# A two-mixer transformer trunk in split fp32: a new order inside mixer B's attention steps

## The chip, the cores and the metric

One core of a Trainium2 chip runs the whole program. The metric is the device time of one execution in microseconds (us); lower is better.

## The reference

The input is a sequence of 1024 tokens of width 1024, and two layers run over it. Layer 0 uses mixer A (attention over a neighbourhood on a grid of tokens), layer 1 uses mixer B (attention with grouped queries: 16 heads of q share 4 heads of k and v). The change is almost wholly in mixer B. Its core, and what surrounds it:

```
for i in range(DEPTH):                       # 2 layers
    h = rms_norm(x, norm_g[i])
    y = mixer_a(h, ...) if i % 2 == 0 else mixer_b(h, ...)
    x = x + y
    g = sigmoid(rms_norm(x, ple_norm_g[i]) @ ple_w_gate[i])
    x = x + g * (p[i] @ ple_w_proj[i])
return rms_norm(x, final_norm_g)

def mixer_b(h, ...):                         # one 128-query block of one head:
    sc = einsum('bkgqd,bksd->bkgqs', qb, k) * scale
    pr = softmax(sc)
    o  = einsum('bkgqs,bksd->bkgqd', pr, v)
    # heads joined, then (o * silu(gate)) @ w_out
```

## The kernel before, in words

Every fp32 factor of a product is split into a high part and a low part, and the products are made with these in fp32r. PE is TensorE, ACT is ScalarE, DVE is VectorE and POOL is GpSimd.

**The steps of mixer B.** Its attention runs through 128 steps, numbered n from 0. A step is one head h, one half hf of the queries and one block t of 128 queries (t from 0 to 3 within a half; the two heads of a pair follow each other). Step n has four pieces:

- `f_S`: four products give the scores of 128 queries against 1024 keys in PSUM (tile `s`, two buffers); then DVE takes the minimum `mn` of each row (the scores have their sign turned).
- `f_E`: ACT makes the exponential of the scores, tile `P` (two buffers), and the row sums.
- `f_T`: PE transposes `P` in two halves of four 128x128 blocks. Each half goes to one of the two PSUM buffers `t`; ACT copies it out as the high part `PTh`, and DVE subtracts to give the low part `PTl`. A buffer `t` is free when its `PTl` is made.
- `f_AV`: for each pair of steps, 16 products of v with the transposed exponentials go into the single PSUM buffer `o`. For each of 8 blocks k of keys there is one with `PTh[:, k]` and one with `PTl[:, k]`; v is the stationary factor in both. At the end of a head (t = 3), `head_end` lists later work: ACT copies half of `o` (line 479), and DVE adds the other half (`join`, line 443), after which the buffer `o` may be written again.

`q_stack` transposes the q of the next pair of heads (four transposes, line 1038) into a buffer `t`; ACT copies it out (line 1040), and later ACT and DVE make the high and low halves `QS` (lines 1047 and 1048). `k_stack` (lines 970 and 973) does the same for k, in steps 48 to 53.

**What sets the order.** The order of each engine's instructions is the order in which the program calls these pieces; each engine takes its own in that order. The loop over `steps` makes a list `att` of pieces, each with a weight. `mix` calls them one by one, and after each it calls `pulse`, which may split another weight (line 217 on ACT, 218 on DVE) and counts down the work that `post` holds for later. After a piece, `mix` also calls dense items (chunks of the projections that fill PE, some 1.4 us each) until their share of all dense work has caught up with the weights so far. So a piece's weight says how much dense work stands behind it. `CB` holds the weights of an even step, `CN` those of an odd one. An even step calls, before the change: `later.tick`, `f_AV` of step n - 1, `f_E` of n + 1, `f_T` of n, `f_S` of n + 2. An odd step calls `later.tick`, `f_T` of n, `f_E` of n + 1, `f_S` of n + 2. `DT` says after how many pulses the last pair of heads has its reciprocals transposed (`across`, line 462), one number for each half hf. In mixer B the transposes use the buffer `o`, in mixer A a buffer `t`.

```
att.append((later.tick, w[0]))
if av:
    att.append((lambda n=n: f_AV(*steps[n - 1]), w[1]))
te = [(lambda n=n: f_T(*steps[n]), w[2])]
if n + 1 < len(steps):
    te.append((lambda n=n: f_E(*steps[n + 1]), w[3]))
if n % 2 == 0:
    te.reverse()
```

Of the kernel before, what the change touches and what calls it, by code (L numbers as in the profile page):

```python
# [21 lines left out]
NT = 8  # L22
# [5 lines left out]
BIG = 1e30  # L28
WSLOTS = 4
CA = (1.0, 0.5, 1.25, 1.0, 0.75)  # L30
CB = (1.25, 1.0, 2.0, 0.5, 1.0)
CN = (1.5, 0.0, 1.0, 1.0, 1.5)
DG, DR, DQ, DY, NP = 1, 2, 2, 1, 8
KT, KN = 2, 4
DO = (2, 3)
DD = ((3, 2), (3, 2))
DT = (5, 2)
FIN = (4, 4)
HOLD = 2
DP = 1  # L40
KD, KS = 3, 4
QD = (2, 5, 8)
QS_AT = 5
QO = (4, 6)
AGE, LAG = 3, 3
YS = (11, 11)
# [108 lines left out]
def trunk(ctx, tc, x, wts, rpb, gains, hgains, mask, rope, out):  # L155
# [145 lines left out]
    def mm(ps, a, b, first, last):  # L301
        pe.matmul(ps, a, b, start=first, stop=last, skip_group_check=True)  # L302
# [554 lines left out]
    def mixer_b(pend):  # L857
        with ExitStack() as es:
# [10 lines left out]
            PTh = one.tile([128, NT, 256], F32R, name="PTh")  # L869
            PTl = one.tile([128, NT, 256], F32R, name="PTl")  # L870
# [9 lines left out]
            KA, KB, V, QT, QST, P, RS, OP = {}, {}, {}, {}, {}, {}, {}, {}  # L880
            later = Later()
# [189 lines left out]
            def f_E(h, hf, t):  # L1071
                ps, mn = P[h, hf, t]
                p = sb.tile([128, 1024], F32, name="P")
                act.activation(p, ps, AF.Exp, bias=mn, scale=-1.0, accum_out=RS[h, hf][:, t:t + 1])  # L1074
                P[h, hf, t] = p

            def f_T(h, hf, t):
                p = P.pop((h, hf, t))
                c = slice((t % 2) * 128, (t % 2) * 128 + 128)
                for b in range(2):  # L1080
                    ps = psT.tile([128, 4, 128], F32, name="t")
                    for i in range(4):
                        k = 4 * b + i
                        pe.transpose(ps[:, i], p[:, k * 128:(k + 1) * 128], ident)  # L1084
                    ks = slice(4 * b, 4 * b + 4)
                    act.activation(PTh[:, ks, c], ps, AF.Copy)  # L1086
                    dve.tensor_tensor(PTl[:, ks, c], ps, PTh[:, ks, c], ALU.subtract)  # L1087
# [4 lines left out]
            def f_AV(h, hf, t):  # L1092
                if t == 1:
                    OP[h, hf] = psO.tile([128, 512], F32, name="o")
                o = OP[h, hf][:, (t - 1) * 128:(t + 1) * 128]
                for k in range(NT):
                    v = V[h // 4][:, k]
                    mm(o, v, PTh[:, k], t == 1 and k == 0, False)
                    mm(o, v, PTl[:, k], False, t == 3 and k == NT - 1)
                if t == 3:  # L1100
                    fin = head_end(sb, h, hf, RS[h, hf], OP.pop((h, hf)), ylive, 1, gg, talloc)
                    if fin:
                        later.add(FIN[1], fin)
# [17 lines left out]
            for g in range(4):  # L1121
                att = []
                for n in range(32 * g, 32 * g + 32):
                    h, hf, t = steps[n]
                    av = n >= 2 and n % 2 == 0
                    w = CB if av else CN
                    att.append((later.tick, w[0]))
                    if av:
                        att.append((lambda n=n: f_AV(*steps[n - 1]), w[1]))
                    te = [(lambda n=n: f_T(*steps[n]), w[2])]  # L1130
                    if n + 1 < len(steps):
                        te.append((lambda n=n: f_E(*steps[n + 1]), w[3]))
                    if n % 2 == 0:
                        te.reverse()
                    att += te
                    if n + 2 < len(steps):
                        att.append((lambda n=n: f_S(*steps[n + 2]), w[4]))
                    m = n + QS_AT
                    if m % 8 == 0 and m < len(steps):
                        hn, fn, _ = steps[m]  # L1140
                        att.append((lambda hn=hn, fn=fn: q_stack(hn // 2, fn), 0.0))
                    if YLOAD_B <= n < YLOAD_B + NT:
                        att.append((lambda t=n - YLOAD_B: load_y(1, t), 0.0))
                if g == 3:
                    att.append((lambda: f_AV(*steps[-1]), CB[1]))
                def gates(p):
                    return [i for hf in range(2) for i in gate_items("bg", p, hf, dalloc, sb, gg)]
                dense = []
                if g > 0:
                    dense += left  # L1150
                if g < 3:
                    qi = q_items(g + 1, pool)
                    kv = kv_items(1, pool) if g == 1 else [None, None]
                    dense += kv[:-2] + qi[:KS] + [k for k in kv[-2:-1] if k] + qi[KS:8] + [k for k in kv[-1:] if k] + gates(2 * g + 1) + qi[8:]
                    left = gates(2 * g + 2)
                else:
                    WQ.cap[3] = 2
                    dense += gates(2 * g + 1) + pp_items(1, dalloc, sb, TAGS_B)
                mix(att, dense, hold=HOLD if g == 3 else 0)
# [169 lines left out]
```

## Time and profile before

| | us |
|---|---|
| runs of the kernel, three | 1572.35, 1569.87, 1572.43 (median 1572.35) |
| the profiled execution | 1569.38 |
| its span, first to last instruction | 1567.6 |
| PE busy in the span | 1522.6 |
| the 128 steps of mixer B, about 791 to 1369 of the span | 578 |

The profiled execution's own time is 1.8 us more than its span, and 3.0 us less than the median of the runs. The clock granted to PE was 0.998 of full over the span, so the kernel runs at the full clock from end to end.

### The profile page before, as it was taken

The numbers are of one execution on the slowest core, as the hardware profiler recorded it, in microseconds if no ns is written. First come the engines' busy times: TensorE is split into PE (matmuls) and PEld (weight loads), VectorE is DVE, ScalarE is ACT, GpSimd is POOL, SyncE is SP. The second block draws the span as 40 slices with busy tenths as digits, with TensorE's granted clock in tenths as the row PEclk, the third lists the DMA queues.
The fourth block names the chain that finished last, engine by engine and source line by source line (L and its number), as shares of the span: only waits on it lengthen the run. The fifth ranks groups of instructions, "written<-read, shape, count | busy, mean of one in ns | idle before, by whom it ended". The sixth has DMA issues, their size and how long they took to land.

```text
span 1567.6 us, 24292 instructions
## 1 busy us (share of the span) xinstructions
PE 1522.6 (97%) x9048; PEld 1328.5 (85%) x9048; DVE 1025.5 (65%) x2062; ACT 871.6 (56%) x1744; POOL 277.3 (18%) x372
## 2 busy tenths in 40 slices
PE   6999999999999999999999999999999999999997
PEld 5888988988988788888988889989899888788886
DVE  6576576477477436547877776777777877625636
ACT  6465465466366522433566776666667767622422
POOL 2111121122112010000312132443132200000023
PEclk9999999999999999999999999999999999999999
DMA  8212122132123972132210111102111213651213
GB/s 273 78 41 74 49 84 78 34 98 78 35 85 95 340 241 67 62 139 90 74 48 21 38 51 41 58 25 68 37 33 42 75 42 112 225 202 54 74 55 128
DMA packets 89861, 138.84 MB, mean 89 GB/s; under 512 B 16912, under 2 KB 55952, under 8 KB 89744
## 3 DMA queue, kind: packets, MB, share of 16 engines
q1 hardware_dynamic: 85136, 122.62, 24.1%
q10 hardware_dynamic: 4608, 14.68, 2.6%
q8 instruction: 71, 1.16, 0.3%
q14 instruction: 46, 0.38, 0.1%
HBM read 104.65 MB, written 36.15 MB: 90 GB/s over the span
## 4 chain that ended last, share of the span: by engine, by line
PE 40%; DVE 7%; ACT 3%; issue 2%; DMA 0%; ACTq 0%; SPq 0%; POOL 0%; DVEq 0%; POOLq 0%
PE d L302 21%; PE o L302 7%; PE t L1084 5%; PE s L302 5%; DVE PTl L1087 2%; DVE mn L1068 1%; ACT PTh L1086 1%; DVE wl L218 1%; PE t L427 1%; ACT wh L217 1%; PE t L1038 0%; ACT P L1074 0%; DVE QS L1048 0%; DVE ss L915 0%; DVE KB L979 0%
## 5 line engine op out<-in xcount | busy, mean ns | idle before, releaser
L302 PE MATMUL d<-wh,HTh 128*128 128x256 f32 (+1 forms) x1096 | 372.5, 340 | 4.6 <-ACT HTh L428 2.1
L302 PE MATMUL d<-wh,HTl 128*128 128x256 f32 (+1 forms) x1096 | 365.8, 334 | 1.6 <-DVE HTl L429 1.5
L302 PE MATMUL d<-wl,HTh 128*128 128x256 f32 (+1 forms) x1096 | 365.3, 333 | 0.0
L1087 DVE TENSOR_TENSOR PTl<-t,PTh 128x512 fp32r<-128x512 f32 x256 | 164.5, 684 | 115.4 <-ACT PTh L1086 114.9
L302 PEld LDWEIGHTS d<-wh,HTh 128*128 128x128 f32 x1096 | 207.9, 190 | 28.0 <-ACT HTh L428 2.7
L302 PEld LDWEIGHTS d<-wh,HTl 128*128 128x128 f32 x1096 | 207.8, 190 | 24.0 <-DVE HTl L429 2.3
L302 PEld LDWEIGHTS d<-wl,HTh 128*128 128x128 f32 x1096 | 208.1, 190 | 21.4
L302 PE MATMUL d<-HTh,wh 128*128 128x512 f32 x504 | 205.9, 409 | 0.0
L302 PE MATMUL d<-HTh,wl 128*128 128x512 f32 x504 | 197.7, 392 | 0.0
L302 PE MATMUL d<-HTl,wh 128*128 128x512 f32 x504 | 197.7, 392 | 0.0
L1074 ACT ACTIVATE P<-s,mn 128x1024 f32<-128x1024 f32 x128 | 142.8, 1115 | 66.2 <-DVE mn L1068 65.1
L302 PE MATMUL o<-PTl,V 128*128 128x256 f32 (+2 forms) x672 | 174.2, 290 | 3.2 <-DVE PTl L1087 2.0
L302 PE MATMUL o<-PTh,V 128*128 128x256 f32 (+2 forms) x672 | 173.0, 288 | 2.3 <-ACT P L1074 1.1
L1086 ACT ACTIVATE PTh<-t 128x512 fp32r<-128x512 f32 x256 | 139.9, 593 | 45.9 <-PE t L1084 45.0
L1068 DVE TENSOR_REDUCE mn<-s 128x1 f32<-128x1024 f32 x128 | 154.8, 1209 | 10.8 <-PE s L302 10.7
L1084 PE MATMUL t<-ident,P 128*128 128x128 f32 x1024 | 137.2, 275 | 8.0 <-DVE PTl L1087 6.6
L218 DVE TENSOR_TENSOR wl<-wstage,wh 128x1024 fp32r<-128x1024 f32 x89 | 115.0, 1298 | 40.9 <-ACT wh L217 40.4
L302 PEld LDWEIGHTS o<-PTl,V 128*128 128x128 f32 x672 | 127.9, 190 | 10.6 <-DVE PTl L1087 6.4
L302 PEld LDWEIGHTS o<-PTh,V 128*128 128x128 f32 x672 | 127.7, 190 | 8.1 <-issue 1.5
L1084 PEld LDWEIGHTS t<-ident,P 128*128 128x128 f32 x1024 | 114.9, 140 | 23.1 <-DVE PTl L1087 16.2
L302 PE MATMUL s<-KA,QS 128*128 128x512 f32 (+2 forms) x384 | 133.6, 402 | 0.0
L302 PE MATMUL s<-KB,QS 128*128 128x512 f32 (+2 forms) x384 | 121.8, 371 | 0.0
(179 smaller groups left out, 2446.8 us busy)
## 6 DMA issues: line engine op xcount, KB each, us to landing
wstage<-in_wts SPq DMA_DIRECT2D x92, 512.0 KB
X<-in_x SPq DMA_DIRECT2D x16, 512.0 KB
pp<-ppD SPq DMA_DIRECT2D x32, 256.0 KB
rb<-rD SPq DMA_DIRECT2D x56, 128.0 KB
ppD<-th SPq DMA_DIRECT2D x20, 256.0 KB
xD<-X SPq DMA_DIRECT2D x8, 512.0 KB
X<-xD SPq DMA_DIRECT2D x8, 512.0 KB
yD0h<-rb SPq DMA_DIRECT2D x14, 256.0 KB
```

Of the source, the lines that this page charges most:

```text
L217: act.activation(hi, s, AF.Copy)
L218: self.rest = lambda: dve.tensor_tensor(lo, s, hi, ALU.subtract)
L302: pe.matmul(ps, a, b, start=first, stop=last, skip_group_check=True)
L427: pe.transpose(ps[:, k], xn[:, (4 * c + k) * 128:(4 * c + k + 1) * 128], ident)
L1068: dve.tensor_reduce(mn, ps, axis=AX.X, op=ALU.min)
L1074: act.activation(p, ps, AF.Exp, bias=mn, scale=-1.0, accum_out=RS[h, hf][:, t:t + 1])
L1084: pe.transpose(ps[:, i], p[:, k * 128:(k + 1) * 128], ident)
L1086: act.activation(PTh[:, ks, c], ps, AF.Copy)
L1087: dve.tensor_tensor(PTl[:, ks, c], ps, PTh[:, ks, c], ALU.subtract)
```

## The change

In an even step the exponential of the next step is called before the products with v. `q_stack` is called one step later than before, directly behind the products with v of an even step, and no longer at the end of an odd step. In `f_AV` all eight products with `PTh` come first and then all eight with `PTl`. The weights of an even step change, so that the dense chunks stand elsewhere. In `DT` the first half's number goes from 5 to 8; this holds for both mixers.

```diff
-CB = (1.25, 1.0, 2.0, 0.5, 1.0)
-CN = (1.5, 0.0, 1.0, 1.0, 1.5)
+CB = (1.25, 0.0, 3.0, 0.5, 1.0)
+CN = (1.5, 1.0, 1.0, 1.5)
-DT = (5, 2)
+DT = (8, 2)
-QS_AT = 5
+QS_AT = 4
...
                 for k in range(NT):
-                    v = V[h // 4][:, k]
-                    mm(o, v, PTh[:, k], t == 1 and k == 0, False)
-                    mm(o, v, PTl[:, k], False, t == 3 and k == NT - 1)
+                    mm(o, V[h // 4][:, k], PTh[:, k], t == 1 and k == 0, False)
+                for k in range(NT):
+                    mm(o, V[h // 4][:, k], PTl[:, k], False, t == 3 and k == NT - 1)
...
-                    h, hf, t = steps[n]
-                    av = n >= 2 and n % 2 == 0
-                    w = CB if av else CN
-                    att.append((later.tick, w[0]))
-                    if av:
-                        att.append((lambda n=n: f_AV(*steps[n - 1]), w[1]))
-                    te = [(lambda n=n: f_T(*steps[n]), w[2])]
-                    if n + 1 < len(steps):
-                        te.append((lambda n=n: f_E(*steps[n + 1]), w[3]))
+                    m = n + QS_AT
+                    later_exp = [lambda n=n: f_E(*steps[n + 1])] if n + 1 < len(steps) else []
+                    turn = lambda n=n: f_T(*steps[n])
                     if n % 2 == 0:
-                        te.reverse()
-                    att += te
+                        fs = [later.tick] + later_exp
+                        w = CB[:len(fs)] if n else (CB[0], CN[2])
+                        if n >= 2:
+                            fs.append(lambda n=n: f_AV(*steps[n - 1]))
+                            w += CB[2:3]
+                        if m % 8 == 0 and m < len(steps):
+                            hn, fn, _ = steps[m]
+                            fs.append(lambda hn=hn, fn=fn: q_stack(hn // 2, fn))
+                            w = w[:-1] + (0.0, w[-1])
+                        fs.append(turn)
+                        w += CB[3:4]
+                    else:
+                        fs = [later.tick, turn] + later_exp
+                        w = CN[:len(fs)]
                     if n + 2 < len(steps):
-                        att.append((lambda n=n: f_S(*steps[n + 2]), w[4]))
-                    m = n + QS_AT
-                    if m % 8 == 0 and m < len(steps):
-                        hn, fn, _ = steps[m]
-                        att.append((lambda hn=hn, fn=fn: q_stack(hn // 2, fn), 0.0))
+                        fs.append(lambda n=n: f_S(*steps[n + 2]))
+                        w += CB[4:] if n % 2 == 0 else CN[3:]
+                    att += zip(fs, w)
```

What it moves on PE, at steps 75 and 76 (in the middle of mixer B; `d` is a dense chunk, `t<-ident,qt` are q's transposes, `o` the products with v, `t<-ident,P` the transposes of an exponential). Before:

```order
L302 MATMUL d<-HTl,wh_10608 128x512
L302 MATMUL d<-HTh,wl_10609 128x512
L1038 MATMUL t<-ident,qt 128x128 x4
L302 MATMUL o<-PTh,V 128x256
L302 MATMUL o<-PTl,V 128x256
L302 MATMUL o<-PTh,V 128x256
L302 MATMUL o<-PTl,V 128x256
```

After the change:

```order
L302 MATMUL d<-HTl,wh_10608 128x512
L302 MATMUL d<-HTh,wl_10609 128x512
L302 MATMUL o<-PTh,V 128x256 x8
L302 MATMUL o<-PTl,V 128x256 x8
L1038 MATMUL t<-ident,qt 128x128 x4
L1084 MATMUL t<-ident,P 128x128 x8
L302 MATMUL s<-KA,QS 128x512 x2
```

The products no longer alternate, and q's transposes have gone from in front of them to behind them, here directly in front of step 76's transposes.

On ACT at steps 67 to 69 (line 1086 copies out a step's transposes, 1074 is an exponential, 1040 copies out q's transposes, 1047 makes the high halves of q, 479 copies out `o`). Before:

```order
L1086 ACTIVATE PTh<-t 128x4x128 x2
L1074 ACTIVATE P,rs<-s,mn 128x1024
L1040 ACTIVATE th<-t 128x512
L1074 ACTIVATE P,rs<-s,mn 128x1024
L1047 ACTIVATE QS<-th 64x512
L1086 ACTIVATE PTh<-t 128x4x128 x2
L479 ACTIVATE Y<-o 64x512
L1047 ACTIVATE QS<-th 64x512
L1086 ACTIVATE PTh<-t 128x4x128 x2
```

After the change:

```order
L1086 ACTIVATE PTh<-t 128x4x128 x2
L1074 ACTIVATE P,rs<-s,mn 128x1024 x2
L1040 ACTIVATE th<-t 128x512
L1086 ACTIVATE PTh<-t 128x4x128 x2
L479 ACTIVATE Y<-o 64x512
L1047 ACTIVATE QS<-th 64x512
L1086 ACTIVATE PTh<-t 128x4x128 x2
L1074 ACTIVATE P,rs<-s,mn 128x1024
L1047 ACTIVATE QS<-th 64x512
```

Both exponentials (68 and 69) now stand in front of q's copy, and the two high halves of q have moved back by one place each.

On PE at the end of mixer B, step 121 (`o<-ident,rb` are the transposed reciprocals of the last pair's first half). Before:

```order
L1084 MATMUL t<-ident,P 128x128 x8
L462 MATMUL o<-ident,rb 128x128 x4
L302 MATMUL s<-KA,QS 128x512 x2
L302 MATMUL s<-KB,QS 128x512 x2
L302 MATMUL o<-PTh,V 128x256
```

After the change:

```order
L302 MATMUL s<-KB,QS 128x512 x2
L302 MATMUL d<-wh_13373,KA 128x512
L302 MATMUL d<-wl_13374,KA 128x512
L302 MATMUL d<-wh_13373,KB 128x512
L302 MATMUL d<-wh_13373,KA 128x512
L302 MATMUL d<-wl_13374,KA 128x512
L302 MATMUL d<-wh_13373,KB 128x512
L462 MATMUL o<-ident,rb 128x128 x4
L302 MATMUL o<-PTh,V 128x256 x8
```

The reciprocals have moved behind the scores and a dense chunk, and now stand directly in front of the products that write the same buffer `o`.

## Rows read from the trace of the kernel before

**Rows 1.** The page: span, and busy time of PE and its weight loads.

```profile
span 1567.6 us, 24292 instructions
PE 1522.6 (97%) x9048; PEld 1328.5 (85%) x9048; DVE 1025.5 (65%) x2062; ACT 871.6 (56%) x1744; POOL 277.3 (18%) x372
```

**Rows 2.** Stages: from:to, length, busy (count) by engine, clock, DMA share, GB/s.

```profile
791.00:1369.00 578.00, 562.62 (x3820) 504.05 (x3819) 430.44 (x686) 407.21 (x753) 138.83 (x216) 1.00 0.19 61
```

**Rows 3.** Waits of weight loads, 791 to 1369: who waited for whom, total, times, longest.

```profile
PEld t L1084 <- DVE PTl L1087: 16.2, 35, 2.1
PEld o L302 <- DVE PTl L1087: 6.4, 15, 1.0
...
PEld t L1038 <- DVE PTl L1087: 1.6, 2, 1.1
...
PEld t L1038 <- POOL Y L514: 1.3, 1, 1.3
```

**Rows 4.** Groups by line, 791 to 1369: busy us, mean ns of one, idle before.

```profile
L302 PE MATMUL o<-PTl,V 128*128 128x256 f32 x511 | 126.6, 286 | 2.7 <-DVE PTl L1087 2.0
L302 PEld LDWEIGHTS o<-PTl,V 128*128 128x128 f32 x511 | 97.4, 191 | 7.4 <-DVE PTl L1087 6.4
```

**Rows 5.** Timeline, products behind step 31: start, length, what, [idle before, releaser].

```profile
926.52 0.28 PE L302 MATMUL o<-PTh,V 128*128 128x256 f32 x1
...
927.49 0.38 PE L302 MATMUL o<-PTl,V 128*128 128x256 f32 x1 [0.69 <-DVE PTl L1087]
...
927.83 0.28 PE L302 MATMUL o<-PTl,V 128*128 128x256 f32 x1
927.95 0.28 PE L302 MATMUL o<-PTh,V 128*128 128x256 f32 x1
```

**Rows 6.** Timeline around the products behind step 21.

```profile
884.04 0.68 DVE L443 SCALAR_TENSOR_TENSOR Y<-o,Y 64x512 f32<-64x512 f32 x1
...
884.87 0.36 PE L302 MATMUL o<-PTh,V 128*128 128x256 f32 x1 [1.12 <-ACT P L1074]
```

**Rows 7.** Timeline, q's transposes behind step 11's scores.

```profile
841.15 1.28 DVE L1087 TENSOR_TENSOR PTl<-t,PTh 128x512 fp32r<-128x512 f32 x2
...
841.89 0.66 PE L1038 MATMUL t<-ident,qt 128*128 128x128 f32 x4 [0.62 <-DVE PTl L1087]
```

**Rows 8.** Timeline, k's transposes directly in front of step 50's.

```profile
1019.82 0.60 PE L970 MATMUL t<-ident,qt 128*128 128x128 f32 x4
1020.25 0.60 PE L1084 MATMUL t<-ident,P 128*128 128x128 f32 x4
1020.51 0.60 ACT L973 ACTIVATE th<-t 128x512 f32<-128x512 f32 x1 [2.01 <-PE t L970]
...
1021.16 0.66 PE L1084 MATMUL t<-ident,P 128*128 128x128 f32 x4 [0.31 <-ACT th L973]
```

**Rows 9.** Groups of ACT by line, 791 to 1369.

```profile
L1074 ACT ACTIVATE P<-s,mn 128x1024 f32<-128x1024 f32 x128 | 142.8, 1115 | 66.2 <-DVE mn L1068 65.1 <-DVE ss L324 0.2
...
L217 ACT ACTIVATE wh<-wstage 128x1024 fp32r<-128x1024 f32 x17 | 17.6, 1049 | 0.0
```

**Rows 10.** Timeline, step 4's last scores and step 5's transposes.

```profile
813.94 0.63 PE L302 MATMUL s<-KB,QS 128*128 128x512 f32 x2
...
814.61 1.15 PE L1084 MATMUL t<-ident,P 128*128 128x128 f32 x7
```

**Rows 11.** Timeline, step 125's transposes.

```profile
1356.49 1.26 PE L1084 MATMUL t<-ident,P 128*128 128x128 f32 x8 [1.27 <-DVE PTl L1087]
```

**Rows 12.** Timeline, step 121: reciprocals and their copy.

```profile
1339.63 0.65 PE L462 MATMUL o<-ident,rb 128*128 128x128 f32 x4 [1.01 <-DVE Y L443]
...
1340.37 0.62 ACT L465 ACTIVATE rb<-o 128x512 f32<-128x512 f32 x1
```

**Rows 13.** Timeline, end of mixer A: reciprocals, then the next products with v.

```profile
532.39 0.60 PE L462 MATMUL t<-ident,rb 128*128 128x128 f32 x4
...
533.74 0.44 PE L302 MATMUL o<-PTh,V 128*128 128x384 f32 x1 [0.75 <-ACT PTh L680]
```

## The prediction

> **What bounds the kernel now.** I read the page first: PE is busy for 97% of the span [rows 1], so time is gained only where PE stops waiting. Then the stages: the 128 steps of mixer B take 578 us, with PE busy for 562.6, DVE for 430 and ACT for 407 [rows 2]. PE is the bound; DVE and ACT, at about 72%, are not, but they hand PE its buffers in a chain (scores, minimum, exponential, transposes, high part, low part), and where the chain is late PE stops. Busy PE hides part of such a stop, because the matmuls overlap; so third I read the waits of the weight loads, which do not overlap in this way [rows 3]. Three kinds of wait are there for the change to move: transposes that wait for a buffer `t`, that is for the low part of the step before (16.2 us in 35 places); products with v that wait for a low part (6.4 us in 15); and q's transposes, for a buffer or for POOL (1.6 and 1.3 us). Together 25.5 us: an order of the pieces that ended all of these waits would gain no more, and a good one gains a part.
>
> The change issues the same instructions with the same shapes, on every engine; SP's and POOL's transfers and their sizes stay as they are. So the sum has only waits in it. How many places there are of each kind I counted in the two orders of PE; the price of one is read from the trace.
>
> **High halves first.** Before, the first product with a low part stands one place behind the first with a high part, and two such products follow each other at 0.12 us [rows 5]. Now it stands eight places behind, 7 x 0.12 = 0.84 us later, and the low part has that long to arrive. Behind step 31 the first low product started 0.97 us after the first high one, instead of 0.12 [rows 5]; with 0.84 us more almost nothing of that would be left. The 6.4 us are 15 waits of 1.0 at most [rows 3], so nearly all of them fit. The fifth high product is now needed 0.48 us earlier than before, but a high part is finished before the low part made from it. I do not take all 6.4: where the low part is late because ACT and DVE themselves are behind, the next transposes need the same two engines and will wait instead. **-5.2** (bounds 0 and -6.4).
>
> *Weights.* The two products of a block k share their v, and the new order parts them. The trace shows 511 weight loads for the 511 low products, 191 ns each, beside the products [rows 4]: v is loaded again even where it is the same, and the pace from low to high (a new v, 927.83 to 927.95 [rows 5]) is 0.12 us. So nothing is lost. [...]
>
> **The buffer `o`.** Behind step 21 the products started only after `join` (884.04 + 0.68 = 884.72), with PE idle for 1.12 us [rows 6]. There one of q's low halves stood on DVE in front of `join`; with `q_stack` a step later it stands behind. **-1.1** (bounds 0 and -1.1).
>
> **q's transposes leave the scores.** In six places before they come straight after the scores of an odd step, four products (0.24 us each [rows 10]) behind that step's own transposes, and must wait for a buffer `t` that its low part frees: behind step 11 that part ended at 841.84 and the transposes began at 841.89, idle 0.62 [rows 7]. Now they come behind the products (16 x 0.12 = 1.9 us later), when that buffer is long free, and POOL too has longer to finish q. **-2.9**, the two rows of q in [rows 3] (bounds 0 and -2.9).
>
> **q's transposes in front of a step's transposes.** This is the price of the former. Counted in the new order, q's transposes stand eight times directly in front of a step's transposes (steps 20, 28, 68, 76, 84, 92, 100 and 116); before, never. They take one of the two buffers, so the second half of the step's transposes must wait for ACT's copy. The nearest rows are k's transposes in front of step 50: the first half began at 1020.25, 0.43 us after k's, but the second at 1021.16, 0.91 after the first, held by a copy of 0.60 us that started as soon as it could [rows 8]. So 0.91 - 0.43 = 0.48 each where ACT is free: 3.8. In step 20, ACT's order has gate copies, an exponential and a weight copy (1.05 us [rows 9]) ahead of q's copy; I add 1.0. **+4.8** (bounds 3.8, and 14 if an exponential of 1.1 us stands ahead each time). k's transposes in front of step 50 get a chunk between: **-0.5**.
>
> **Steps with nothing between.** Where an even step's transposes, the scores and the odd step's transposes follow without a dense chunk, the buffers come free too late. Between steps 4 and 5 the last two scores start at 813.94 and 0.24 us apart, so the transposes could start at 814.42 and did at 814.61 [rows 10]; with 0.1 for the second half I call this 0.3. There are 8 such places before and 12 after: +1.2. But step 125, which waited 1.27 us [rows 11], is no longer one of them: a chunk of 1.4 us (12 products at 0.12) moves in front of it, -1.1. **+0.1** (bounds -1.1 and +1.2).
>
> **The exponential in front of the products.** It is an ACT instruction and the products are PE's, so it takes no PE time. In most steps ACT's order does not change by it at all; what changes is that q's copy and one of q's high halves no longer delay it. The copy-out of the next transposes can then only be earlier. I give it nothing (bounds: the second rival below, and -1).
>
> **Last reciprocals later.** In mixer B, step 121, they waited 1.01 us for `join` [rows 12]; three pulses later they don't: -1.0. But now the products that write the same single buffer `o` stand straight behind them, and must wait for ACT's copy. Before, the scores (four products) lay between and hid it: copy from 1340.37 to 1340.99 [rows 12]. In the new order of ACT an exponential stands ahead of this copy. So: 0.62 for the copy; 0.3 until it starts (0.74 behind the first transpose, of which 0.43 are PE's own time [rows 8, 12]); 1.1 for the exponential [rows 9]; 0.5 for its own wait for a minimum (65.1 us over 128 exponentials [rows 9]): 2.5 in all, net **+1.5** (bounds -0.1, if the exponential is past, and +1.9). In mixer A the transposes (4 x 0.11 = 0.43 us) lay in a stretch in which PE then waited 0.75 us for a high part anyway [rows 13]; moved behind it, they are no longer hidden: **+0.4** (bounds 0 and 0.9).
>
> **Sum.** -5.2 - 1.1 - 2.9 + 4.8 - 0.5 + 0.1 + 1.5 + 0.4 = -2.9 us. The profiled execution took 1569.4 us, so 1566.5. Of the three runs one lies near it (1569.87) and two at 1572.4; the median stands 3.0 us above the profiled one. I do not know where the next runs will fall, and put the forecast between 1566.5 and 1569.5, at 1568.
>
> **Rivals.**
> - *More is gained.* The bounds at the good end: low halves -6.4, reciprocals -0.1, step 20 at 0.48 like the others: -6.4 - 1.1 - 2.9 + 3.8 - 0.5 + 0.1 - 0.1 + 0.4 = -6.7, 1562.7 us. For it: the low halves' longest wait is 1.0. Against it: ACT's order in steps 20 and 123. Chance 0.20.
> - *The waits only move.* Half of what high halves first and the earlier `join` save comes back in front of the next transposes, since the low part that was late is the one that frees their buffer: -2.9 + 3.2 = +0.3, 1569.7 us. For it: 35 waits of transposes for that very release, against 15 of the products [rows 3]. Against it: mostly a dense chunk lies between. Chance 0.17.
> - *Slower: the early exponential holds ACT.* It stands at the head of ACT's queue until its minimum is there (65.1 us of such waits [rows 9]), and q's copy now stands behind it, with the second half of the next transposes, their high part and their low part behind that. If PE reaches q's transposes before the exponential has even begun, each of the eight places pays 1.1 us more: -2.9 + 8 x 1.1 - 1.0 = +4.9, 1574.3 us; where ACT also has a weight copy there, more. [...] It decides from 0.8 us more in each place: that makes +0.2%. Chance 0.17.
> - *Weights held.* If a pair did share v, all 512 low products would need a load more, and at 191 ns a load against a pace of 120 each would cost 0.07 us: +36 us, 1605. [...] Against it are 511 loads in 511 products [rows 4]. Chance 0.02.
>
> **Chances.** The forecast's own case (-6 to 0) has 0.44. What this kernel's measurement can tell from no change is about 0.2%, 3.1 us; the forecast lies on that edge, so half of its case counts as faster and half as the same. Faster 0.22 + 0.20 = 0.42, the same 0.22 + 0.17 = 0.39, slower 0.17 + 0.02 = 0.19. The likeliest case's own range is 1564 to 1571. The wider one reaches from the first rival (1562.7, less a little) to the slower one (1574.3, plus part of the 3 us between runs): 1561 to 1576.
>
> **What would show it.** High halves first: the waits of `o` loads for `PTl` fall from 6.4 us to under 1.5. q: no wait of q's transposes for `PTl` or POOL is left, and in its place the second half of steps 20, 28, 68, 76, 84, 92, 100 and 116 waits for line 1040, about 0.5 us each. Reciprocals: no wait for `join` at line 462, but 1 to 3 us of the products behind it for line 465. Waits moved: the 16.2 us of transposes for `PTl` grow. The prediction is wrong if ACT's waits for `mn` grow much and appear behind q's transposes, if the scores wait for `QS` (made a step later now), or if the pace of the products is no longer 0.12 us.

## The result, and the profile after

The changed kernel takes 1576.88 us (median of 6 runs, 1575.93 to 1579.89) against 1571.56 (6 runs, 1569.77 to 1573.78) for the kernel before on the same chip: ratio 1.0039, 95% interval 1.0028 to 1.0050. It is slower by 0.4%, where 1568 and "faster" were forecast. The profiled execution took 1576.70 us.

The page, beside [rows 1]: the span is 7.3 us longer, and PE is busy for only 1.2 us more.

```profile
span 1574.9 us, 24278 instructions
PE 1523.8 (97%) x9048; PEld 1328.3 (84%) x9048; DVE 1024.9 (65%) x2062; ACT 872.5 (55%) x1744; POOL 275.9 (18%) x372
```

The stages, beside [rows 2] (from:to, length, busy time and count by engine, clock, DMA share, GB/s): in 586 us, PE gets through 3829 instructions, nine more than before in 578.

```profile
791.00:1377.00 586.00, 565.08 (x3829) 505.05 (x3828) 430.58 (x692) 408.65 (x754) 137.33 (x216) 1.00 0.19 60
```

The clock is as before (0.998 of full over the span, in both), so the time is lost in waits, in mixer B. From the first transpose of a step to the last, the kernel before took 571.9 us (the first line) and this one 578.6 (the second):

```profile
L1084 PE MATMUL t<-ident,P x1024: 270/272/330, 794.4 to 1366.3; 128*128 128x128 f32 x171
L1084 PE MATMUL t<-ident,P x1024: 269/273/330, 795.5 to 1374.1; 128*128 128x128 f32 x171
```

(count, shortest/median/longest in ns, first and last start). Of the 7.3 us of span 6.8 lie here (6.7 by these rounded figures).

The waits of the weight loads in mixer B, beside [rows 3] (who waited for whom, total us, times, longest):

```profile
PEld t L1084 <- DVE PTl L1087: 26.8, 55, 2.0
PEld t L1084 <- ACT th L1040: 6.1, 8, 1.4
PEld o L302 <- ACT rb L465: 3.5, 1, 3.5
PEld o L302 <- ACT PTh L1086: 1.6, 3, 0.7
PEld o L302 <- DVE PTl L1087: 1.2, 1, 1.2
PEld t L970 <- POOL Y L514: 0.8, 1, 0.8
```

What was to go has gone: the products' wait for low parts fell from 6.4 to 1.2, q's transposes wait no more. But the transposes' wait for the low part of the step before grew from 16.2 us in 35 places to 26.8 in 55, they now wait 6.1 for q's copy in the eight places foreseen, and the last reciprocals' copy holds the products for 3.5. A wait of a load is not all lost time, since loads run ahead of their products (at step 84 of this trace the load waited 1.36 us, and PE itself stood idle for 1.12), so sizes below come from the starts of PE's instructions: the distance from one to the next, less the median distance of the same two kinds in the kernel before, added up.

The timeline shows the three kinds of new stop (start, length, what, [idle before, releaser]; lines of other work between these are left out).

```profile
920.38 1.03 PE L1084 MATMUL t<-ident,P 128*128 128x128 f32 x8
920.58 0.38 ACT L950 ACTIVATE qt<-d 128x256 f32<-128x256 f32 x1 [0.26 <-PE d L302]
921.00 0.42 ACT L914 ACTIVATE t<-qt 128x256 f32<-128x256 f32 x1
921.32 1.07 ACT L1086 ACTIVATE PTh<-t 128x512 fp32r<-128x512 f32 x2
921.71 0.64 PE L302 MATMUL s<-KB,QS 128*128 128x512 f32 x2
921.93 1.29 DVE L1087 TENSOR_TENSOR PTl<-t,PTh 128x512 fp32r<-128x512 f32 x2 [1.54 <-ACT PTh L1086]
922.68 1.26 PE L1084 MATMUL t<-ident,P 128*128 128x128 f32 x8 [0.33 <-DVE PTl L1087]
...
1181.10 1.11 ACT L1074 ACTIVATE P<-s,mn 128x1024 f32<-128x1024 f32 x1 [1.96 <-DVE mn L1068]
1181.13 0.60 PE L1084 MATMUL t<-ident,P 128*128 128x128 f32 x4
1182.21 0.59 ACT L1040 ACTIVATE th<-t 128x512 f32<-128x512 f32 x1
1182.85 0.66 PE L1084 MATMUL t<-ident,P 128*128 128x128 f32 x4 [1.12 <-ACT th L1040]
...
1347.56 0.60 PE L462 MATMUL o<-ident,rb 128*128 128x128 f32 x4
1349.65 1.11 ACT L1074 ACTIVATE P<-s,mn 128x1024 f32<-128x1024 f32 x1 [1.24 <-DVE mn L1068]
1350.75 0.59 ACT L465 ACTIVATE rb<-o 128x512 f32<-128x512 f32 x1
1351.39 1.21 PE L302 MATMUL o<-PTh,V 128*128 128x256 f32 x8 [3.23 <-ACT rb L465]
```

First, step 31: its transposes follow step 30's with only the scores between. They could start 0.47 behind 921.71 and start at 922.68, 0.50 late, where the mildest place [rows 10] had 0.2: two small copies of ACT stand in front of step 30's copies. Second, step 84: the second half starts 1.72 behind the first, since an exponential stands ahead of q's copy and ACT waited 1.96 for its minimum. Third, step 121: the copy of the reciprocals stands behind an exponential whose minimum is late.

The second stop is longer here than the order alone makes it. The minimum was late because the instruction of DVE ahead of it (line 527, part of the gate) took 1.63 us, while POOL's product at line 514, which starts when a transfer lands, ran beside it:

```profile
1176.90 1.29 POOL L514 TENSOR_TENSOR Y<-Y,rb 128x512 f32<-128x512 f32 x1 [6.05 <-DMA rb<-rD]
1177.11 1.63 DVE L527 SCALAR_TENSOR_TENSOR G<-th,G 128x512 f32<-128x512 f32 x1 [0.94 <-ACT th L523]
```

In after_dt_back (below), whose order at step 84 is the same, POOL's product began 0.9 us later, behind this instruction of DVE, which took 0.69:

```profile
1176.58 0.69 DVE L527 SCALAR_TENSOR_TENSOR G<-th,G 128x512 f32<-128x512 f32 x1 [0.94 <-ACT th L523]
1177.78 1.30 POOL L514 TENSOR_TENSOR Y<-Y,rb 128x512 f32<-128x512 f32 x1 [7.44 <-DMA rb<-rD]
```

There step 84 is 0.41 us late, as most of the eight places are, and not 1.28. What the order itself shows of this kind is step 100, 0.83 late in both.

### The profile page after: what moved, and what is told of

The parts are those of the page before. It is cut to its first block, busy times and chain, and to the rows that moved or that the text cites. A ratio compares the mean times of both kernels' runs of the same rounds, so it can differ in the third digit from the quotient of the medians.

```text
span 1574.9 us, 24278 instructions
## 1 busy us (share of the span) xinstructions
PE 1523.8 (97%) x9048; PEld 1328.3 (84%) x9048; DVE 1024.9 (65%) x2062; ACT 872.5 (55%) x1744; POOL 275.9 (18%) x372
## 4 chain that ended last, share of the span: by engine, by line
PE 40%; DVE 7%; ACT 4%; issue 2%; DVEq 0%; ACTq 0%
PE d L302 21%; PE o L302 7%; PE t L1084 6%; PE s L302 5%; DVE PTl L1087 2%; DVE mn L1068 1%; DVE wl L218 1%; ACT PTh L1086 1%; ACT P L1074 1%; PE t L427 1%; ACT wh L217 1%; ACT th L523 0%; ACT G L522 0%; DVE KB L979 0%; ACT th L1040 0%
## 5 line engine op out<-in xcount | busy, mean ns | idle before, releaser
L1084 PE MATMUL t<-ident,P 128*128 128x128 f32 x1024 | 140.7, 276 | 15.5 <-DVE PTl L1087 10.2
L1084 PEld LDWEIGHTS t<-ident,P 128*128 128x128 f32 x1024 | 114.2, 140 | 37.9 <-DVE PTl L1087 26.8
L302 PE MATMUL o<-PTh,V 128*128 128x256 f32 (+2 forms) x672 | 118.1, 287 | 5.4 <-ACT rb L465 3.2
L302 PE MATMUL o<-PTl,V 128*128 128x256 f32 (+2 forms) x672 | 119.4, 289 | 1.4 <-DVE PTl L1087 1.0
L681 DVE TENSOR_TENSOR PTl<-t,PTh 128x384 fp32r<-128x384 f32 (+1 forms) x128 | 66.5, 520 | 74.8 <-ACT PTh L680 73.7
L302 PEld LDWEIGHTS d<-HTh,wl 128*128 128x128 f32 x504 | 94.6, 188 | 21.8
```

Of the source, the lines that this page charges most:

```text
L681: dve.tensor_tensor(PTl[:, sl], ps[:, :m], PTh[:, sl], ALU.subtract)
```

## The experiments

Theory after the result: the time is lost where transposes stand too close to others, either behind a step's transposes with nothing between (a dense chunk has left) or behind q's transposes. Rival: the exponential in front of the products, which I had costed at nothing, holds ACT. Each kernel was timed against the kernel before on the same chip; ratios are to that kernel, with 95% intervals.

### One part alone, on the kernel before

**High halves first** (the diff's lines in `f_AV` and nothing else).

> The kernel before with one part of the change alone: in the products with v the eight high halves come first. Theory 1 (each wait is local, and the change is the sum of its places): in the profiles of before and of the changed kernel the products' waits for low parts fall from 5.4 us to 1.3; alone it should give -4 to -6 us against before, with the transposes of steps 73 and 89 waiting some 0.4 us each more. Theory 2 (the waits only move to the next transposes): 0 to -1.5 us, and the transposes' wait for PTl grows by what the products lose.

Measured: 1567.18 us, ratio 0.9975 (0.9965 to 0.9985). The waits in mixer B:

```profile
PEld t L1084 <- DVE PTl L1087: 21.0, 46, 2.1
...
PEld o L302 <- ACT PTh L1086: 1.5, 3, 0.6
```

The products' 6.4 us of waits for low parts are gone altogether. But the transposes wait 4.8 us more for that same release, so the rival of the moved waits holds for about half: by PE's starts 5.2 us went at the low parts and 0.5 at the high ones, and 3.0 came back at odd steps' transposes. That leaves 2.7, and the spans differ by 2.8 (1567.6 and 1564.8).

**The exponential in front.**

```diff
-    att.append((lambda n=n: f_AV(*steps[n - 1]), w[1]))
+    if n + 1 < len(steps):
+        att.append((lambda n=n: f_E(*steps[n + 1]), 0.0))
+    att.append((lambda n=n: f_AV(*steps[n - 1]), w[1] + w[3]))
...
-    if n + 1 < len(steps):
+    if n + 1 < len(steps) and not av:
         te.append((lambda n=n: f_E(*steps[n + 1]), w[3]))
```

> The kernel before with the exponential of the next step alone called before the products with v, all dense chunks left where they were on PE. Theory 1: no wait on PE depends on it, 0 within 1.5 us. Theory 3 (the early exponential holds ACT at the head of its queue): +2 to +6 us, with ACT's waits for mn grown and PE's transposes waiting longer.

Measured: 1577.39 us, ratio 1.0043 (1.0030 to 1.0055), with PE's order unchanged, except that the last reciprocals now stand behind step 121's scores, directly in front of the products (0.7 us of the loss by PE's starts). As large as the whole loss, so the rival had to be followed up (below).

**The dense chunks behind the products.**

```diff
-CB = (1.25, 1.0, 2.0, 0.5, 1.0)
+CB = (1.25, 1.0, 0.5, 2.0, 1.0)
```

> The kernel before with the new place of the dense chunks alone: behind the products with v and no longer behind the even step's transposes (weights 0.5 for the transposes, 2.0 for what is called just before them). Steps with no chunk between the even and the odd transposes: 19, where before has 8. Theory 1: 11 more such places at about 0.35 us, +3 to +5 us, all of it in front of the odd steps' transposes. Theory 3 (the early exponential made the changed kernel slow, the chunks' place costs nothing): within 1.5 us of before.

Measured: 1582.10 us, ratio 1.0071 (1.0058 to 1.0084), more than either expectation. Odd steps with nothing between cost 13.0 us instead of 6.6; the products' waits for high and low parts grew by 1.7 each.

**q's transposes behind the products.** `QS_AT` is 4, and `q_stack` is called behind `f_AV` of an even step; in 14 places it stands directly in front of a step's transposes.

> The kernel before with q's transposes alone moved behind the products with v (one step later). With the old weights they then stand directly in front of a step's transposes in 14 places. Theory 1: 14 x 0.48 and some 2 us more where ACT has an exponential or a weight copy ahead, less 2.4 us that they waited behind the scores, less about 1.5 us at the products behind step 21, 29 and 101: +3 to +6 us. Theory 2 (waits only move): +1 us or less, the step's second half waits but the next transposes wait less.

Measured: 1581.20 us, ratio 1.0068 (1.0054 to 1.0081), more than either expectation. Transposes wait 7.0 us for q's copy, in 14 places, and 26.6 instead of 16.2 for low parts: the exponential, still called behind the products, now stands behind q's copy, and so the odd step is late as well.

**Last reciprocals later** (`DT = (8, 2)`).

> The kernel before with the later reciprocals alone (8 in place of 5 pulses for the first half of the last pair). Theory 1: in mixer B they wait 1.25 us less and the products behind them about 2.5 to 3.5 us more, in mixer A 0.4 us more: +1.5 to +3 us. If the changed kernel's 3.5 us wait there came from the other parts (the exponential in front, the chunks), it is within 1 us of before.

Measured: 1572.00 us, ratio 1.0004 (0.9996 to 1.0013): nothing. By PE's starts the reciprocals are 1.0 less late, and the products behind them 1.0 more.

By their ratios the five alone come to -3.9 + 6.8 + 11.2 + 10.7 + 0.6 = +25 us, and together to +6. They do not add: each changes what stands beside the others.

### One part undone, in the changed kernel

**Reciprocals back** (`DT = (5, 2)`).

> The changed kernel with the first half's reciprocals back at 5 pulses. They then stand behind step 123's scores and in front of a dense chunk. Theory 1: the 3.5 us wait of the products behind them goes, and 0.4 us in mixer A: -3 to -4 us against the changed kernel, +2 to +3 us against before. If ACT and DVE set the pace there, less than 1 us.

Measured: 1573.45 us, ratio 1.0017 (1.0008 to 1.0026). This gives 3.4 us back. By PE's starts the stop of step 121 is gone (3.5), and the reciprocals wait 1.0 for `join` again; another 0.9 is step 84, where the order is the same (above). In dt_alone the reciprocals stand directly in front of the products too, and these are only 1.0 later. There PE stood idle for 0.75 us until the reciprocals' copy, and in the changed kernel for 3.23: the exponential ahead of the copy waited for its minimum and began 2.09 behind the reciprocals' transposes (1347.56 and 1349.65). The later reciprocals are the one part whose undoing helps.

**Dense chunks back between the transposes** (`CB = (1.25, 0.0, 1.5, 2.0, 1.0)`).

> The changed kernel with the dense chunks put back behind the even step's transposes (weights 1.25, 0, 1.5, 2.0, 1.0). Places with nothing between fall from 19 to 7, but q's transposes stand directly in front of a step's transposes in 14 places, where the changed kernel has 8. Theory 1: -12 x 0.35 - 1 (step 105) + 6 x 0.5 = about -2 us against the changed kernel, +4 us against before. Theory 3 (early exponential): as slow as the changed kernel, +6 us.

Measured: 1576.82 us, ratio 1.0032 (1.0020 to 1.0045), no gain. The waits tell why:

```profile
PEld t L1084 <- DVE PTl L1087: 18.6, 38, 2.1
PEld t L1084 <- ACT th L1040: 9.9, 14, 1.5
```

The transposes' wait for low parts falls from 26.8 to 18.6, but with less dense work behind the products q's transposes stand directly in front of a step's in 14 places instead of 8. By PE's starts: -6.4 and +5.7.

**Exponential back behind the products.**

```diff
-    fs = [later.tick] + later_exp
+    fs = [later.tick] + (later_exp if n < 2 else [])
...
+    if n >= 2 and later_exp:
+        fs += later_exp
+        w = w + (0.0,)
     fs.append(turn)
```

> The changed kernel with one thing undone: the next exponential is issued behind the products and q's transposes again; PE's order of pieces is the same. Theory (with q's transposes behind the products the exponential must stand in front of them, else it waits behind q's copy and everything behind it is late, as in q_alone): 3 to 5 us slower than the changed kernel. Rival (the early exponential is a pure loss in every order, as exp_alone alone would suggest): 4 to 6 us faster than the changed kernel.

Measured: 1596.88 us, ratio 1.0166 (1.0152 to 1.0180): 20 us slower than the changed kernel, the theory's side and far beyond its size. Waits, then the timeline of ACT at step 5:

```profile
PEld t L1084 <- DVE PTl L1087: 45.8, 70, 2.8
```

```profile
811.58 0.60 ACT L1040 ACTIVATE th<-t 128x512 f32<-128x512 f32 x1 [1.53 <-PE t L1038]
...
813.76 1.10 ACT L1074 ACTIVATE P<-s,mn 128x1024 f32<-128x1024 f32 x1
...
815.59 1.09 ACT L1086 ACTIVATE PTh<-t 128x512 fp32r<-128x512 f32 x2
```

Without the early exponential ACT stands idle 1.53 us until q's transposes come, copies q, waits another 0.84 for a dense chunk, makes that chunk's two copies, and only at 813.76 begins the exponential; the copies of step 4's transposes come behind it at 815.59. This order puts the exponential behind q's copy and also behind the chunks that the change moved behind the products, and the run does not tell the two apart. So the early exponential is what makes the new places of q and of the chunks bearable, and is not what makes the changed kernel slow as a whole, though at step 121 it stands ahead of the reciprocals' copy. What it costs there this run cannot show, because the reciprocals themselves stand in front of a dense chunk in it.

**q back behind the scores** (`q_stack` at the end of an odd step, as before, with `QS_AT` at 5).

> The changed kernel with q's transposes back behind the scores of the step before. The 6.6 us of transposes held by q's copy go, 3 us of q's transposes behind the scores come back, and ACT's copy to rb stands behind the early exponential again as in exp_alone (3.5 us). Theory: these cancel, within 2 us of the changed kernel. Rival (only the places of q count): 3.5 us faster than the changed kernel.

Measured: 1584.62 us, ratio 1.0086 (1.0072 to 1.0099). Both expectations missed: it is 7.7 us slower than the changed kernel. No transposes wait for q's copy, but up to 1376 us they wait 32.9 us in 67 places for low parts (26.8 in 55 in the changed kernel): odd steps with nothing between rise from 12.0 to 16.4, where ACT's copies (q's high halves, and `rb`, next) now fall in front of them. This reading is from the trace; no run of its own tested it.

### Why the early exponential costs something alone

At step 22 of the kernel before, while the exponential of step 23 waits for its minimum, ACT has just made a copy for the work that follows the attention, the high part of `Y` (line 510, tile `rb`; lines of other work are left out here and below):

```profile
884.77 0.62 ACT L510 ACTIVATE rb<-Y 128x512 fp32r<-128x512 f32 x1
887.86 1.12 ACT L1074 ACTIVATE P<-s,mn 128x1024 f32<-128x1024 f32 x1 [2.47 <-DVE mn L1068]
888.97 1.08 ACT L1086 ACTIVATE PTh<-t 128x512 fp32r<-128x512 f32 x2
```

The same place in exp_alone:

```profile
889.14 1.12 ACT L1074 ACTIVATE P<-s,mn 128x1024 f32<-128x1024 f32 x1 [3.14 <-DVE mn L1068]
890.25 0.62 ACT L510 ACTIVATE rb<-Y 128x512 fp32r<-128x512 f32 x1
890.77 1.08 ACT L1086 ACTIVATE PTh<-t 128x512 fp32r<-128x512 f32 x2
...
892.25 1.25 PE L1084 MATMUL t<-ident,P 128*128 128x128 f32 x8 [0.32 <-DVE PTl L1087]
```

The exponential is now issued first, so the copy waits behind it: ACT is idle 0.7 us longer, and the copies of the transposes start 1.6 us behind the exponential's start instead of 1.1. By PE's starts six odd steps (15, 23, 31, 79, 95 and 111) are some 0.7 late each, where the kernel before loses 0.06 at most. To test it, only the split of `Y` was issued one pulse earlier, that is this copy and DVE's subtraction behind it (line 511):

```diff
-YS = (11, 11)
+YS = (11, 10)
```

> The kernel before with the exponential in front of the products, as in exp_alone, and in addition the split of Y (ACT's copy to rb, 0.62 us) of the stage behind is issued one pulse earlier, so that it stands ahead of the early exponential in ACT's queue again. PE's order is the same as in exp_alone. Theory (the loss of exp_alone is this copy, which no longer runs while the exponential waits for its minimum but only behind it): the six waits of 0.6 us in steps 15, 23, 31, 79, 95 and 111 go, so 3.5 us less than exp_alone, about 2.5 us above before. Rival (it is the exponential itself that holds the copies of the transposes): the same as exp_alone, 6 us above before.

Measured: 1573.07 us, ratio 1.0020 (1.0011 to 1.0028), 4.3 us less than exp_alone. At step 22:

```profile
886.11 0.62 ACT L510 ACTIVATE rb<-Y 128x512 fp32r<-128x512 f32 x1
889.34 1.12 ACT L1074 ACTIVATE P<-s,mn 128x1024 f32<-128x1024 f32 x1 [2.62 <-DVE mn L1068]
890.45 1.08 ACT L1086 ACTIVATE PTh<-t 128x512 fp32r<-128x512 f32 x2
```

The copy is ahead again, and the transposes wait less for low parts in all of mixer B (exp_alone, then exp_rb_ahead):

```profile
PEld t L1084 <- DVE PTl L1087: 23.6, 51, 2.1
PEld t L1084 <- DVE PTl L1087: 17.2, 37, 2.0
```

So the copy was most of the price: by PE's starts 4.5 of exp_alone's 6.5 us went with it. The other 2.0 stay (0.7 of them at the last reciprocals), and this kernel is still slower than the one before. No run moved the split without the early exponential, but in the kernel before those six steps have nothing to gain. In the changed kernel `q_stack` brings one more pulse ahead of the next step, and there the copy comes early enough by itself: it is ahead of the exponential in all 14 places, and behind it in all 14 of after_q_back and of best_mid_q (next), where that pulse falls elsewhere or is gone.

### Orders that keep the gains

**q between the high and the low products**, in the changed kernel with chunks and reciprocals back (`mid` is `q_stack`, called between the two loops of `f_AV`).

```diff
...
+    if mid:
+        mid()
     for k in range(NT):
         mm(o, V[h // 4][:, k], PTl[:, k], False, t == 3 and k == NT - 1)
...
```

> The changed kernel with the chunks put back, the reciprocals back at 5 pulses, and q's transposes between the eight high and the eight low products, so that 0.96 us of products stand on either side of them. No q directly in front of transposes, none directly behind scores, 7 places with nothing between. Theory 1: of the waits of before remain the bare places (6 us), the others in front of odd transposes (7 us) and under 2 us at the products: -8 to -11 us against before. Theory 2 (waits only move): -2 us or less. Theory 3: slower than before, as the early exponential is kept.

Measured: 1570.78 us, ratio 0.9998 (0.9989 to 1.0006). A miss: eight low products are too few to hide q's copy (transposes still wait 5.7 us for it, in 7 places), and the pulse that had kept the copy to `rb` early is gone.

**The same with `YS = (11, 10)`.**

> best_mid_q with the split of Y one pulse earlier, as in exp_rb_ahead, so that the copy to rb stands ahead of the early exponential. Theory: the waits of steps 23, 31, 79 and 95 go, 3 us less than best_mid_q, about 1568. Rival (the copy is only late by chance of this order): the same as best_mid_q.

Measured: 1567.00 us, ratio 0.9978 (0.9969 to 0.9987): 3.8 less by the medians and 3.0 by PE's starts, as the theory has it.

**High halves first, and q directly in front of the products**, on the kernel before; no other part of the change. The lines in `f_AV` are those of hi_alone.

```diff
-QS_AT = 5
+QS_AT = 4
...
     att.append((later.tick, w[0]))
+    m = n + QS_AT
+    if m % 8 == 0 and m < len(steps):
+        hn, fn, _ = steps[m]
+        att.append((lambda hn=hn, fn=fn: q_stack(hn // 2, fn), 0.0))
     if av:
         att.append((lambda n=n: f_AV(*steps[n - 1]), w[1]))
...
```

> The kernel before with high halves first, and with q's transposes issued directly in front of the products with v instead of behind the scores of the step before; exponential, chunks and reciprocals as before. Between q's transposes and the next transposes of P then lie 16 products (1.9 us), so neither waits for the other's buffer. Theory: the 3.0 us of q's transposes behind the scores go and nothing comes in their place: 2 to 3 us below hi_alone, at 1564 to 1565. Rival (the waits only move, to the next transposes or to their high parts, behind q's two copies on ACT): the same as hi_alone.

Measured: 1564.60 us, ratio 0.9960 (0.9948 to 0.9973): faster than both kernels, and 2.6 us below hi_alone by the medians (2.2 by PE's starts; the intervals of the two ratios overlap), as expected. Its waits:

```profile
PEld t L1084 <- DVE PTl L1087: 22.1, 46, 2.0
...
PEld t L1038 <- DVE PTl L1087: 0.6, 1, 0.6
PEld o L302 <- DVE PTl L1087: 0.4, 1, 0.4
```

Nothing waits for q's copy, q's transposes hardly wait, the products neither. With this order the two dearest parts could be priced without q in the way.

**The chunks behind the products, here** (`CB = (1.25, 1.0, 0.5, 2.0, 1.0)`; 19 odd steps with nothing between instead of 8).

> hi_q_front with the dense chunks moved behind the products, as the change does (odd steps with nothing between: 19 instead of 8; q's transposes still have the products behind them, so they hold no transposes of P). Theory (a step with nothing between costs PE 0.3 to 0.5 us by itself): 11 places by 0.5, 5 to 6 us slower than hi_q_front, about the time of before. Rival (the 11 us of wts_alone came mostly from low parts and q, which are cured here): within 2 us of hi_q_front.

Measured: 1572.47 us, ratio 1.0011 (1.0003 to 1.0020): 7.9 us more, on the theory's side and above its size. By PE's starts those odd steps cost 15.8 instead of 6.9, that is 0.8 for each of the 11 new places. Five of these (15, 23, 27, 31 and 111) had lost 2.9 together with a chunk still in between, so that taking the chunk away cost 0.5 a place. The products' waits grew by 2.2.

```profile
PEld t L1084 <- DVE PTl L1087: 28.7, 54, 2.0
```

**The exponential in front, here** (the edit of exp_alone).

> hi_q_front (before, high halves first, q's transposes directly in front of the products) and in addition the next exponential in front of q's transposes and the products; PE's order is the same. Theory (the early exponential gains nothing where no copy of q stands between it and the scores, and costs the copies of ACT that used to run while it waits): 3 to 6 us slower than hi_q_front, with new waits of about 0.6 us in odd steps. Rival (in the best order the early exponential is free, and only its company in the change was bad): the same as hi_q_front within 1.5 us.

Measured: 1566.22 us, ratio 0.9972 (0.9961 to 0.9982), 1.6 us more, and the spans differ by 0.7 (1563.0 and 1563.7); the intervals overlap. At the last reciprocals, which have moved as in exp_alone, 0.7 are lost by PE's starts. The theory of 3 to 6 us fell. In this order of ACT the copy to `rb` stands ahead of the exponential in all 14 places, which is why the loss of exp_alone does not come. The exponential by itself costs next to nothing, and gains nothing.

## Why the prediction was wrong

By the terms of its sum, with what PE's starts in mixer B give for each (us; before, after):

| term | forecast | measured |
|---|---|---|
| products wait for low parts | -5.2 | -4.1 (5.4, 1.3) |
| products wait for high parts or `join` | -1.1 | -2.1 (3.2, 1.1) |
| q's transposes behind scores (the 0.6 are k's, held by POOL) | -2.9 | -2.4 (3.0, 0.6) |
| transposes directly behind q's or k's | +4.3 | +6.0 (0.6, 6.6) |
| odd steps with nothing between | +0.1 | +5.4 (6.6, 12.0) |
| odd steps with a chunk between | 0 | +1.8 (6.9, 8.7) |
| last reciprocals, mixer B | +1.5 | +2.2 (1.3, 3.5) |
| sum in mixer B | -3.3 | +6.8 |

**Steps with nothing between** is the step that failed. I counted 12 such places after the change; there are 19 (steps 1, 5, 9, 13, 17, 21, 23, 25, 27, 29, 31, 57, 59, 61, 105, 107, 109, 111 and 113) against 8. And the price of 0.3 was too low, even for the place where I read it [rows 10]: by PE's starts it costs 0.44, since its transposes are also slower from one to the next (1.25 us for step 5's eight, against 1.04 for step 4's). In other places ACT's own copies fall in between (step 31 above), and the 13 places that are new cost from 0.26 to 0.73, 0.5 on the mean. A right count at my price would have made 11 x 0.3 - 1.1 = +2.2, and turned the sum from -2.9 to -0.8. The price made up most of the rest; 1.2 is step 105, which had nothing between in either order and rose from 0.45 to 1.64. It did so in every kernel with the change's order, also with chunks, q or exponential put back, and in none made from the kernel before; why stays open. hi_q_front_wts shows the chunks' new place with q out of the way, 7.9 us, of which odd steps make 5.6.

**The exponential in front of the products** was costed at nothing, and in the changed kernel that is right: hi_q_front_exp prices it at 0.7 to 1.6, after_exp_back shows that the new places of q and of the chunks need it, exp_rb_ahead that most of its cost alone is a copy that falls behind it. I had written that ACT's order hardly changes by it; that missed the copy to `rb`, which this kernel escapes only by q's extra pulse. The slower rival (1574.3) named the exponential, with the time nearly right, but that is luck: its mechanism shows in two of the eight places only. Steps 84 and 100 are 1.28 and 0.83 late, with the exponential ahead of q's copy, and most of step 84's is a slow instruction of DVE in this execution (above). Step 20 pays 1.25 for a weight copy, as I had foreseen, and the other five 0.41 to 0.47.

**High halves first** was right in mechanism and too large in net effect. By itself it brings 2.7 of the 5.2 (3.6 in the medians), because the rival of the moved waits is half true: without their stop at the products, odd steps' transposes come earlier and wait for the same low parts. Of the +1.8 of odd steps with a chunk between, which I had at nothing, 0.8 are of this kind: steps 73 and 89 are 0.4 later each in hi_alone as in the changed kernel. Step 121 (1.2) is the largest of the others; its cause is not settled. In reading the waits of loads I had also taken it that loads do not overlap as products do. They do: in the changed kernel the 512 loads for low parts, 192 ns each, add up to 98 us and keep the load path busy for 66.0. The rival of held weights is dead: before and after, 512 loads stand beside the 512 products with low parts, so no pair has one load; in hi_alone, as in the changed kernel, the products with low parts load v each time, at 191 and 192 ns, as in [rows 4], and hi_alone is faster.

**q** went as foreseen in both directions: what was saved behind the scores (2.4) was more than lost again in front of the transposes. The gain was to be had without the loss, with q in front of the products (hi_q_front).

**Last reciprocals** were under-sized in mixer B: a stop of 3.5 us where I had 2.5. I gave the exponential in front of the copy 0.8 until it starts; it was 1.7 (1349.65 less 1347.99, when the products could have begun), the rest fits. after_dt_back gives back 3.4, of which 2.5 lie at this place. In mixer A the wait for the high part grew from 0.75 [rows 13] to 1.40 while 0.43 of PE's work left the place in front of it, so 0.2 were lost there, where I had 0.4.

## What to carry to other kernels

Where two buffers go round between a producer and a chain of copies, let a program count the places in which two producers follow each other with nothing between, for the order before and after, and price them at the mean of all such places, not at the mildest. Before an instruction that waits is issued earlier, list what else on its engine now comes behind it: a cheap copy that ran during the wait loses its free place, and moving that copy by one place may undo the cost (here a copy of 0.62 us in 14 places, and 4.3 of 6.8 us). Parts of a reordering do not add (here +25 alone, +6 together), so the useful experiment is one part on an order in which the others do no harm; it found a kernel at 0.9960 with one of the five ideas as it was and another with q in a better place.

## What the runs showed that I had not expected

Issuing the copies to `rb` on ACT (14 of 0.62 us in mixer B), an engine busy for 55% of the span, and their subtractions on DVE one pulse earlier changed the whole kernel by 4.3 us in one order and 3.8 in another. And the same early exponential is worth +6 us in the order before, +1.6 in the best one and -20 in the changed kernel (where without it the exponential would also stand behind the chunks), with the same instructions on every engine: in this kernel the price of an instruction's place is a property of its neighbours.
